# Making the high and low parts of a projection's weights in two halves of four blocks each

## The chip, the cores and the metric

The kernel runs on one core of one Trainium2 chip. The metric is device time of one execution in microseconds, here as the median of several runs; lower is better. TensorE (PE) multiplies, VectorE (DVE) and ScalarE (ACT) do elementwise work, GpSimd (POOL) does some of it, and SyncE (SP) issues most of the DMAs.

## The reference

One block of a sequence model in fp32, with 1024 positions of width 1024 and a depth of 1:

```
hn = rms_norm(x, norm_mix_g)
u = hn @ w_in                                  # 1024 x 7864
u_mla, u_fox, u_ssm, u_gate = split(u)
y_a = mla_branch(u_mla, ...) @ w_br_mla        # 8 heads, latent attention
y_b = fox_branch(u_fox, ...) @ w_br_fox        # 8 heads, attention with a forget gate
y_c = ssm_branch(u_ssm, ...) @ w_br_ssm        # conv of xBC, state space scan, 16 heads
g = sigmoid(u_gate + b_gate).reshape(B, S, 3, D)
merged = g[:, :, 0] * y_a + g[:, :, 1] * y_b + g[:, :, 2] * y_c
x = x + merged @ w_out
x = x + conv_ffn(rms_norm(x, norm_ffn_g), ...) # two projections of width 2816, a conv, a gate
```

## The kernel before, in words

**Products of fp32.** Each fp32 operand is split into a high part in fp32r and a low part, the raw value minus the high part, and a product is made of three matmuls: high by high, high by low, low by high. For weights, ACT copies the raw tile `wr` to the high tile `wh`, and DVE subtracts, `wl = wr - wh`.

**Stages.** Up to about 389 us the kernel normalises the input and makes those columns of `hn @ w_in` that the attention needs. Then the 16 attention heads run, up to about 908 us, and the chunks of the state space scan (SSD), up to about 1113 us. Branch outputs, merge, `w_out` and the feed-forward block follow.

**The fill.** The columns of `w_in` that attention doesn't need (12 blocks of 128 columns for the convolution, 24 for the gates) are projected by `all_fill` (L1157 to L1189). A block is two halves of 24 matmuls, 128x512 (L1174), into two alternating PSUM tiles `mm`; then ACT takes the result, with a plain copy (L1179) for a convolution block or a tanh (L1153) for a gate. The convolution's taps `t` follow on DVE (L1132 and others). The fill's matmuls are dealt out between those of the attention heads, and later between those of the SSD chunks, two of the eight k-blocks at a time, by `merge` and `advance`, which always advance the stream that is least far.

**The weights of a block.** `fill_load` (L1108 to L1119) is called for block n + 1 when block n starts. It issues the load of 128x1024 values (eight k-blocks of 128) into one of two `wr` tiles, and takes one of two `wh` and `wl` tiles. For blocks 0 and 1 the split is made at once. For the other 34 the copy (L1117) and the subtraction (L1118) are put into a queue with due times.

**The queue.** The order of all engines in these stages is written by a clock of costs: each step of a stream adds its estimated TensorE time to `clk`. `later(us, fn)` puts an instruction in the queue, due `us` after the present clock; `run_until` emits those that are due, by their due time; `force(h)` emits the queue up to handle `h`, when a buffer is wanted again or a block's weights are needed. `rl[0]`, which `fill_load` returns, is the handle of the last step that reads the raw tile and is forced before the block's matmuls. `pin` keeps an instruction in this order against its neighbours that are pinned too; the compiler's scheduler places the rest, so that a change of one step can swap others.

**What stands around it.** In attention, per row of 128 queries: scores `s` (L1291) into three alternating PSUM tiles; row maxima `nmx` (L1296 for a first chunk, L1307 for the last, L1309 joins two) on DVE; exponentials `pm` (L1314) on ACT; the row sum's reciprocal (L1319, L1320) on DVE, and the normalisation (L1321) on POOL. The probabilities are transposed (`tp`, L1379), copied by ACT to high parts `pth` (L1384) and by DVE to low parts `ptl` (L1385), and multiplied with the values into `o` (L1344 to L1352). ACT copies half of `o` out (L1357), and DVE adds the other half (L1362), which frees the PSUM region that the next values write. In the SSD chunks PE transposes through one PSUM tile `stp` (x at L1516, y at L1620); ACT copies it out (`xT` L1517, `yT` L1621), makes the decays `E` (L1548, L1549) and their high parts `Eh` (L134), and DVE the low parts `El` (L135) for the products `py` (L1584).

Of the kernel before, what the change touches and what calls it, by code (L numbers as in the profile page):

```python
# [15 lines left out]
AF = mybir.ActivationFunctionType  # L16
# [21 lines left out]
def f32(ap):  # L38
    return ap.bitcast(F32)
# [3 lines left out]
def block_kernel(ctx: ExitStack, tc: tile.TileContext, x, positions, norm_mix_g, w_in, b_gate,  # L43
# [5 lines left out]
    V, A, G, T, SY = nc.vector, nc.scalar, nc.gpsimd, nc.tensor, nc.sync  # L49
# [77 lines left out]
    def uid(s):  # L127
        cnt[0] += 1
        return f"{s}_{cnt[0]}"

    def split(h, l, src, he=None, le=None):
        he = he or A
        le = le or V
        i = A.activation(h, src, AF.Copy) if he is A else he.tensor_copy(h, src)  # L134
        return i, le.tensor_sub(l, src, f32(h))  # L135
# [8 lines left out]
    def pin(ins):  # L144

        i = ins.ins
        if i.engine in tail:
            tc.add_manual_dep(i, tail[i.engine],
                              mybir.DependencyInfo(mybir.DependencyClass.NoSync, mybir.DependencyReason.DATA),
                              reason="pin")  # L150
        tail[i.engine] = i.name
        return ins
# [918 lines left out]
    def later(us, fn):  # L1071
        h = [clk[0] + us, uid(""), fn]
        queue.append(h)
        return h
# [31 lines left out]
    pin = tc.keep_in_program_order  # L1106

    def fill_load(c0, now=False):  # L1108
        raw, rl = f_wr.get()
        SY.dma_start(raw, w_inv[:, :, c0:c0 + P])  # L1110
        h, _ = f_wh.get()
        l, _ = f_wl.get()
        if now:
            split(h, l, raw)
            rl[0] = None
            return h, l, rl
        later(4.0, lambda: pin(A.activation(h, raw, AF.Copy)))  # L1117
        rl[0] = later(5.3, lambda: pin(V.tensor_sub(l, raw, f32(h))))  # L1118
        return h, l, rl  # L1119

    def conv_done(j, u, ul, t0):
# [35 lines left out]
    def all_fill():  # L1157

        conv = [("c", j, C_XBC + j * P) for j in range(12)]
        gates = [(b, j, C_G + b * D + j * P) for b in (1, 0, 2) for j in range(NK)]  # L1160
        blocks = [e for n in range(12) for e in (conv[n], gates[n])] + gates[12:]
        nxt = fill_load(blocks[0][2], True)
        for n, (kind, j, c0) in enumerate(blocks):
            wh, wl, rl = nxt
            if n + 1 < len(blocks):
                nxt = fill_load(blocks[n + 1][2], n == 0)
            force(rl[0])
            u, ul = f_t4.get()
            for half in range(2):
                ps, pl = f_ps.get()  # L1170
                hs = slice(512 * half, 512 * half + 512)
                for k in range(NK):
                    for i, (a, b) in enumerate(((wh, hnh), (wh, hnl), (wl, hnh))):
                        T.matmul(ps, a[:, k, :], b[half][:, k, :], start=(k == 0 and i == 0),  # L1174
                                 stop=(k == NK - 1 and i == 2))
                    if (k + 1) % grain[0] == 0 and k < NK - 1:
                        yield 0.65 * grain[0]
                if kind == "c":
                    fn = lambda ps=ps, hs=hs, u=u: A.activation(u[:, hs], ps, AF.Copy)  # L1179
                else:  # L1180
                    fn = lambda ps=ps, hs=hs, u=u, r=8 * kind + j: gate_tanh(u[:, hs], ps, pc_g[:, r:r + 1])
                wait = 50.0 if n == len(blocks) - 1 and half == 1 else 0.0
                pl[0] = later(wait + 1.4, fn)
                if half == 1:
                    if kind == "c":
                        conv_done(j, u, ul, 2.2)
                    else:
                        ul[0] = later(wait + 2.0, lambda u=u, g=g_d[kind][j]: SY.dma_start(g, u))
                yield 0.65 * grain[0]  # L1189
# [461 lines left out]
    with ExitStack() as pe_:  # L1651
# [9 lines left out]
        def ops_tile(i):  # L1661
            return [mps[i // 4].tile([P, S], F32R, name=uid(n), tag=f"{n}{i}") for n in ("ah", "al")]

        for b, wsrc, nk in ((1, w_br_fox, 4), (0, w_br_mla, 4), (2, w_br_ssm, 8)):
# [3 lines left out]
            for k in range(nk):  # L1668
                if b == 1 and k < 2:
                    raw = frp.tile([P, 2, 512], F32, name=uid("ar"), tag=f"ws{k}").rearrange("p a s -> p (a s)")  # L1670
                else:
                    raw = fpl.tile([P, S], F32, name=uid("ar"), tag="t4", bufs=4)
                i = SY.dma_start(raw, ys_d[k] if b == 2 else att_d[b][k * P:k * P + P, :])
                if b == 1 and k < 2:
                    behind_(i, ys_stores[4])
                if b == 1:
                    h, l = fox_hl[k]
                else:
                    h, l = ops_tile(4 + k if b == 0 else k)
# [140 lines left out]
    for nh in range(2):  # L1820
        hl = []
        for kk in range(2):
            h, l = (ops[4 if nh else 2 * kk + i].tile([P, 4, 512], F32R, name=uid(n), tag=f"{n}{nh}{kk}")
                    for i, n in enumerate(("woh", "wol")))
            hl.append((h, l))
            for k in range(0, 4, 2):
                late = nh == 0 and kk == 1
                raw = fpl.tile([P, 2, 512], F32, name=uid("raw"), tag="t4" if late else "wr", bufs=4 if late else 2)
# [26 lines left out]
    for t, nh in units:  # L1855
        ns = slice(512 * nh, 512 * nh + 512)
        if nh == 0 and 4 <= t < 4 + FIRST:
# [10 lines left out]
            else:  # L1868
                raw = fpl.tile([P, NK, P], F32, name=uid("wr"), tag="t4", bufs=4)
# [249 lines left out]
    for pi, name in enumerate(steps):  # L2119
# [6 lines left out]
        for k in range(NFH):  # L2126
# [14 lines left out]
            for m, j in todo:  # L2141
                h, l = loaded[pi * NFH + j]
# [55 lines left out]
```

## Time and profile before

| | |
|---|---|
| runs | 2030.01, 2022.77, 2022.13 us |
| median of the runs | 2022.77 us |
| the profiled execution | 2026.82 us, its span 2025.1 us, mean granted clock 0.997 |
| busy: PE, DVE, ACT, POOL | 1997.5, 1382.0, 934.8, 651.1 us |
| DMA | 304.13 MB, mean 150 GB/s |

The profile is of one execution. The span runs from its first to its last recorded instruction; the execution's own time has 1.7 us around it. Rows of the timeline give start and duration in microseconds from the span's start, then engine, line, operation, output and inputs by the program's names. An instruction's duration can overlap the next one's start, so the distance between two starts is what one costs its engine in a row of them. Idle time ahead of an instruction stands in brackets with what released it. "PEclk" is the granted TensorE clock as a share of full speed.

### The profile page before, as it was taken

Reading aid. Unit: us, or ns where it says so; the run is one execution under the profiler, and the core shown is the slowest. Engines: PE = TensorE matmul, PEld = TensorE weight load, DVE = VectorE, ACT = ScalarE, POOL = GpSimd, SP = SyncE. Lnnn points to the kernel's source line nnn. Section 1 sums busy time; section 2 is a strip of 40 time slices with the busy share of each in tenths; the row PEclk is TensorE's granted clock in tenths of the full one; section 3 lists DMA queues with packets and bytes.
Section 4 is the critical chain, followed back from the end, with each engine's and each line's share of the span. In section 5 each row is a group of like instructions: output and inputs, shape, how many; then the busy total and the mean of one; then the engine's idle time right before and its main releaser. Section 6 shows DMA issues by size and latency. Waiting matters only on the chain. (4 is left out here: it accounts for less than half of the span.)

```text
span 2025.1 us, 28777 instructions
## 1 busy us (share of the span) xinstructions
PE 1997.5 (99%) x10189; PEld 1681.6 (83%) x10189; DVE 1382.0 (68%) x2410; ACT 934.8 (46%) x1700; POOL 651.1 (32%) x640
## 2 busy tenths in 40 slices
PE   8999999999999999999999999999999999999999
PEld 8999788888888888888777878888778888888887
DVE  7777567267666676657885556558997777675665
ACT  5555323255555556546665222324454444454432
POOL 5133322021222322213332063100555444522655
PEclk9999999999999999999999999999999999999999
DMA  6166857543535445424443678342322211249575
GB/s 176 51 193 217 267 174 217 170 125 102 140 116 140 125 112 155 116 74 142 131 137 128 220 243 291 136 135 83 115 87 90 84 63 42 84 137 329 204 259 193
DMA packets 276539, 304.13 MB, mean 150 GB/s; under 512 B 19070, under 2 KB 209546, under 8 KB 276395
## 3 DMA queue, kind: packets, MB, share of 16 engines
q1 hardware_dynamic: 276392, 302.29, 48.2%
q8 instruction: 80, 1.31, 0.3%
q14 instruction: 65, 0.52, 0.1%
q10 hardware_dynamic: 2, 0.00, 0.0%
HBM read 209.04 MB, written 93.19 MB: 149 GB/s over the span
## 5 line engine op out<-in xcount | busy, mean ns | idle before, releaser
L1321 POOL TENSOR_SCALAR pm<-pm,rs 128x128 f32<-128x128 f32 (+7 forms) x128 | 105.8, 829 | 415.4 <-DVE rs L1320 294.2
L1174 PE MATMUL mm<-hnh,wh 128*128 128x512 f32 x576 | 238.0, 413 | 0.0
L1174 PE MATMUL mm<-hnh,wl 128*128 128x512 f32 x576 | 226.5, 393 | 0.0
L1174 PE MATMUL mm<-hnl,wh 128*128 128x512 f32 x576 | 226.3, 393 | 0.0
L2145 PE MATMUL dn<-dr,dr 128*128 128x512 f32 x592 | 182.3, 389 | 0.0
L1314 ACT ACTIVATE pm<-s,nmx 128x128 f32<-128x128 f32 (+2 forms) x192 | 110.4, 581 | 65.3 <-DVE nmx L1309 61.8
L2145 PEld LDWEIGHTS dn<-dr,dr 128*128 128x128 f32 x592 | 111.1, 188 | 23.1
L1174 PEld LDWEIGHTS mm<-hnh,wl 128*128 128x128 f32 x576 | 108.4, 188 | 24.9
L1174 PEld LDWEIGHTS mm<-hnl,wh 128*128 128x128 f32 x576 | 109.2, 190 | 16.4 <-issue 0.5
L1174 PEld LDWEIGHTS mm<-hnh,wh 128*128 128x128 f32 x576 | 109.2, 190 | 16.3 <-issue 0.7
L1385 DVE TENSOR_TENSOR ptl<-tp,pth 128x512 fp32r<-128x512 f32 (+1 forms) x160 | 98.4, 632 | 33.0 <-ACT pth L1384 30.8
L1384 ACT ACTIVATE pth<-tp 128x512 fp32r<-128x512 f32 (+1 forms) x160 | 84.8, 555 | 72.6 <-PE tp L1379 72.5
L2145 PE MATMUL dn<-dr 128*128 128x512 f32 x296 | 115.2, 389 | 0.0
L135 DVE TENSOR_TENSOR dr<-dr,dr 128x1024 fp32r<-128x1024 f32 x52 | 75.3, 1459 | 48.3 <-ACT dr L134 35.6
L188 PE MATMUL ybr<-al,wh 128*128 128x512 f32 x256 | 99.4, 390 | 1.2 <-DVE al L1682 1.0
L188 PE MATMUL ybr<-ah,wh 128*128 128x512 f32 x256 | 98.9, 390 | 1.1 <-ACT ah L1681 0.9
L188 PE MATMUL ybr<-ah,wl 128*128 128x512 f32 x256 | 98.9, 390 | 0.0
L1307 DVE TENSOR_REDUCE nmx<-s 128x1 f32<-128x384 f32 (+3 forms) x128 | 65.8, 518 | 32.8 <-PE s L1291 19.2
L134 ACT ACTIVATE dr<-dr 128x1024 fp32r<-128x1024 f32 x52 | 54.8, 1061 | 71.6 <-PE dn L2145 55.0
L1379 PE MATMUL tp<-ident,pm 128*128 128x128 f32 x576 | 79.8, 273 | 0.6 <-POOL pm L1321 0.6
L135 DVE TENSOR_TENSOR wl<-S,wh 128x1024 fp32r<-128x1024 f32 x42 | 63.2, 1504 | 23.5 <-ACT wh L134 23.5
L134 ACT ACTIVATE wh<-wr 128x1024 fp32r<-128x1024 f32 (+1 forms) x40 | 35.0, 876 | 93.9 <-PE ybr L188 47.1
(528 smaller groups left out, 5853.3 us busy)
## 6 DMA issues: line engine op xcount, KB each, us to landing
dr<-act_d SPq DMA_DIRECT2D x99, 256.0 KB
wr<-in_w_in_dram SPq DMA_DIRECT2D x36, 512.0 KB
g_d<-t SPq DMA_DIRECT2D x24, 512.0 KB
gl<-g_d SPq DMA_DIRECT2D x24, 512.0 KB
wr<-in_ffn_w_up_dram SPq DMA_DIRECT2D x23, 512.0 KB
ws<-in_ffn_w_down_dram SPq DMA_DIRECT2D x22, 512.0 KB
wsum_d<-ws SPq DMA_DIRECT2D x22, 512.0 KB
act_d<-fa SPq DMA_DIRECT2D x22, 512.0 KB
```

The costliest lines, as they stand in the source:

```text
L134: i = A.activation(h, src, AF.Copy) if he is A else he.tensor_copy(h, src)
L135: return i, le.tensor_sub(l, src, f32(h))
L188: T.matmul(ps, a(k), b(k), start=(i == 0), stop=(i == n - 1))
L1174: T.matmul(ps, a[:, k, :], b[half][:, k, :], start=(k == 0 and i == 0), stop=(k == NK - 1 and i == 2))
L1307: V.reduce_max(nmx[:, ci:ci + 1], ps[:, :b - a], axis=AX, negate=True)
L1314: pss[cj][1][0] = later(t0 + 0.9 + 0.1 * cj, lambda cj=cj, a_=a_, b_=b_: A.activation(p_[:, a_:b_], pss[cj][0][:, :b_ - a_], AF.Exp, bias= ...
L1321: G.tensor_scalar(p_[:, 0:n * P], p_[:, 0:n * P], rs[:, 3:4], 0.0, op0=ALU.mult, op1=ALU.add)
L1379: T.transpose(pt[:, off:off + P], pn[qi][0][:, k * P:k * P + P], ident)
L1384: later(cs + 0.05, lambda th=th, pt=pt, off=off: A.activation(th[:, :off], pt[:, :off], AF.Copy))
L1385: pl[0] = later(cs + 0.6, lambda th=th, tl=tl, pt=pt, off=off: V.tensor_sub(tl[:, :off], pt[:, :off], f32(th[:, :off])))
L2145: T.matmul(ps[m], a[:, ts_], b[:, 512:], start=first_ and j == 0 and q == 0, stop=j == NFH - 1 and q == 2, skip_group_check=not first_)
```

## The change

The copy and the subtraction of a block's weights are each made in two halves of four k-blocks (512 of the 1024 values of a partition). The copies are due at +4.0 and +5.2 us of the order's clock and the subtractions at +5.0 and +6.2 us; `rl[0]` is the second subtraction. The loads, tiles and matmuls are the same, and so are the splits of blocks 0 and 1.

```
-        later(4.0, lambda: pin(A.activation(h, raw, AF.Copy)))
-        rl[0] = later(5.3, lambda: pin(V.tensor_sub(l, raw, f32(h))))
+        for i in range(2):
+            ks = slice(4 * i, 4 * i + 4)
+            later(4.0 + 1.2 * i, lambda ks=ks: pin(A.activation(h[:, ks, :], raw[:, ks, :], AF.Copy)))
+            rl[0] = later(5.0 + 1.2 * i, lambda ks=ks: pin(V.tensor_sub(l[:, ks, :], raw[:, ks, :], f32(h[:, ks, :]))))
```

After the change the copy is L1119, the subtraction L1120, and lines behind them have numbers that are higher by two. The steps move on their engines as follows. The first place is at about 541 us of the profile of before, in the attention stage. ACT before (the outputs are the high weights `wh`, output halves `o` and probabilities `pm`):

```order
L1314 ACTIVATE pm_6452,rs_6454<-s_6455,nmx_6453 128x512
L1314 ACTIVATE pm_6452,rs_6454<-s_6498,nmx_6453 128x384
L1117 ACTIVATE wh_6481<-wr_6479 128x1024
L1357 ACTIVATE o_1675_6525<-o 64x256
L1357 ACTIVATE o_1684_6552<-o 64x256
L1314 ACTIVATE pm_6513,rs_6515<-s_6516,nmx_6514 128x512
L1314 ACTIVATE pm_6513,rs_6515<-s_6543,nmx_6514 128x512
L1384 ACTIVATE pth_6576<-tp_6571 128x512
L1384 ACTIVATE pth_6583<-tp_6578 128x512
```

ACT in the same place after the change (each name's last number is another, since more names are drawn):

```order
L1316 ACTIVATE pm_6464,rs_6466<-s_6467,nmx_6465 128x512
L1316 ACTIVATE pm_6464,rs_6466<-s_6510,nmx_6465 128x384
L1119 ACTIVATE wh_6493<-wr_6491 128x512
L1359 ACTIVATE o_1689_6537<-o 64x256
L1119 ACTIVATE wh_6493<-wr_6491 128x512
L1359 ACTIVATE o_1698_6565<-o 64x256
L1386 ACTIVATE pth_6590<-tp_6585 128x512
L1386 ACTIVATE pth_6597<-tp_6592 128x512
L1316 ACTIVATE pm_6525,rs_6527<-s_6528,nmx_6526 128x512
L1316 ACTIVATE pm_6525,rs_6527<-s_6556,nmx_6526 128x512
```

The first copy of `o` stands behind half a split and ahead of the other half, and the two `pth` copies now stand ahead of the two exponentials of 128x512.

DVE at that place before, from a tap of the convolution on (`nmx` are row maxima, `o` the sum of the two output halves, `t` taps):

```order
L1132 SCALAR_TENSOR_TENSOR t_1624_6440<-t_1545_6238,pc_g,t_1624_6440 128x512
L1307 TENSOR_REDUCE nmx_6514<-s_6543 128x1
L1362 TENSOR_TENSOR o_1676_6526<-o,o_1675_6525 64x256
L1118 TENSOR_TENSOR wl_6482<-wr_6479,wh_6481 128x1024
L1309 TENSOR_TENSOR nmx_6514<-nmx_6514 128x1
L1132 SCALAR_TENSOR_TENSOR t_1624_6440<-t_1545_6238,pc_g,t_1624_6440 128x510
L1307 TENSOR_REDUCE nmx_6564<-s_6566 128x1
L1362 TENSOR_TENSOR o_1685_6553<-o,o_1684_6552 64x256
```

DVE there after the change:

```order
L1134 SCALAR_TENSOR_TENSOR t_1636_6452<-t_1557_6248,pc_g,t_1636_6452 128x512
L1364 TENSOR_TENSOR o_1690_6538<-o,o_1689_6537 64x256
L1120 TENSOR_TENSOR wl_6494<-wr_6491,wh_6493 128x512
L1309 TENSOR_REDUCE nmx_6526<-s_6556 128x1
L1120 TENSOR_TENSOR wl_6494<-wr_6491,wh_6493 128x512
L1309 TENSOR_REDUCE nmx_6578<-s_6580 128x1
L1364 TENSOR_TENSOR o_1699_6566<-o,o_1698_6565 64x256
L1311 TENSOR_TENSOR nmx_6526<-nmx_6526 128x1
```

The first sum comes ahead of the row maximum that stood before it, one maximum stands between the two half subtractions, and the joined maximum (`nmx` from `nmx`) comes last of these.

The second place is at about 1031 us, in an SSD chunk. ACT before (`E` are decays, `yT` the transposed output of the chunk):

```order
L134 ACTIVATE Eh_12188<-E_12184 128x512
L1153 ACTIVATE t_3862_12156<-mm_12157,pc_g 128x512
L134 ACTIVATE Eh_12206<-E_12202 128x512
L1548 ACTIVATE E_12214<-pse_12211 128x512
L1621 ACTIVATE yT_12023<-stp_12246 128x512
L1549 ACTIVATE E_12214<-E_12214 128x512
```

ACT there after the change:

```order
L134 ACTIVATE Eh_12248<-E_12244 128x512
L1155 ACTIVATE t_3924_12216<-mm_12217,pc_g 128x512
L134 ACTIVATE Eh_12267<-E_12263 128x512
L1119 ACTIVATE wh_12214<-wr_12212 128x512
L1550 ACTIVATE E_12275<-pse_12272 128x512
L1623 ACTIVATE yT_12083<-stp_12308 128x512
L1551 ACTIVATE E_12275<-E_12275 128x512
```

The second half of a block's copy stands between a copy of `Eh` and the decay ahead of `yT`; before, the whole copy stood eleven rows above the first of these.

## The prediction

> **What bounds the kernel now.** I read the busy line of the page first, then a table of stages, then what TensorE waited for in the two stages that the change touches, and last the places of those waits in the timeline. The busy line:
>
> ```profile
> PE 1997.5 (99%) x10189; PEld 1681.6 (83%) x10189; DVE 1382.0 (68%) x2410; ACT 934.8 (46%) x1700; POOL 651.1 (32%) x640
> ```
>
> TensorE is busy for 99% of the span. The fill, in whose course all the changed splits stand, runs from 389.4 to 1112.6 us, as one row of the fill's own line shows (count, shortest, median and longest ns, first and last start):
>
> ```profile
> L1174 PE MATMUL mm<-hnh,wh x576: 387/396/796, 389.4 to 1112.6; 128*128 128x512 f32 x192
> ```
>
> It has an attention stage, to 908 us, and an SSD stage. The rows of the table of stages (start and end, length, then busy time of PE, its weight loads, DVE, ACT and POOL, granted clock, DMA share, GB/s):
>
> ```profile
> 389.00:908.00 519.00, 515.25 (x3033) 440.22 (x3031) 341.06 (x793) 285.96 (x707) 121.75 (x143) 1.00 0.45 123
> 908.00:1113.00 205.00, 201.60 (x1041) 162.01 (x1042) 153.38 (x249) 125.05 (x202) 63.22 (x80) 0.99 0.43 133
> ```
>
> TensorE stands still for 519.00 − 515.25 = 3.75 us in attention and 205.00 − 201.60 = 3.40 us in SSD. No edit to VectorE or ScalarE work can give back more than about these 7.2 us, so the question is which of them the splits cause. The waits of TensorE by releaser (total us, times, longest), attention first, then SSD:
>
> ```profile
> PE o L1344 <- DVE o L1362: 1.6, 1, 1.6
> PE s L1291 <- ACT pm L1314: 0.9, 1, 0.9
> PE tp L1379 <- POOL pm L1321: 0.6, 1, 0.6
> ```
>
> ```profile
> PE stp L1516 <- ACT yT L1621: 1.5, 2, 1.2
> PE stp L1516 <- DVE o L1362: 0.9, 1, 0.9
> PE py L1584 <- ACT E L1548: 0.8, 1, 0.8
> PE stp L1620 <- ACT y L1612: 0.7, 1, 0.7
> ```
>
> Each is a single event or two. No row names a split (`wh`, `wl`) as what TensorE waited for. A split can cause such a wait only by standing ahead of the named instruction on its engine.
>
> **The fixed cost of two halves.** Groups of the whole run (operation, shapes, count, busy us, mean ns of one, idle time before):
>
> ```profile
> L1117 ACT ACTIVATE wh<-wr 128x1024 fp32r<-128x1024 f32 x34 | 35.9, 1055 | 0.0
> L1118 DVE TENSOR_TENSOR wl<-wr,wh 128x1024 fp32r<-128x1024 f32 x34 | 41.7, 1226 | 1.0 <-ACT wh L1117 1.0
> L134 ACT ACTIVATE Eh<-E 128x512 fp32r<-128x512 f32 x32 | 20.0, 628 | 12.3 <-DVE E L1550 11.3 <-PE py L1584 0.9
> L135 DVE TENSOR_TENSOR El<-E,Eh 128x512 fp32r<-128x512 f32 x32 | 21.9, 688 | 6.8 <-ACT Eh L134 6.2
> ```
>
> The last two are the same operations at the new size. A pair of half copies takes 2 x 628 − 1055 = 201 ns more than one whole copy, a pair of half subtractions 2 x 688 − 1226 = 150 ns more: over 34 blocks 6.8 us more on ACT and 5.1 us more on DVE. Both lie beside matmuls: in the attention row ACT is busy for 286 of 519 us and DVE for 341. I cost them at nothing except where the engine is saturated just ahead of a wait; if the cover were gone, 201 + 150 = 351 ns a block would be exposed, 34 x 0.351 = 11.9 us in all. On this the Trainium skill, page "VectorE: DVE Perf Modes", section "The TRN2 errata", speaks against the change: one large tile pays the access latency once, many small ones pay it per tile, and by its formula for an fp32 tensor_tensor the halves would take 691 ns each against 1224 ns; the rows above agree within 3 ns, and by its price the DVE term would be 158 ns a block, 5.4 us over 34.
>
> **The second half is later.** Its copy is due at +5.2 us and its subtraction at +6.2 us of the order's clock, where the whole ones had +4.0 and +5.3. The block with the least room, in one row of DVE and one of PE:
>
> ```profile
> 899.39 1.22 DVE L1118 TENSOR_TENSOR wl<-wr,wh 128x1024 fp32r<-128x1024 f32 x1
> ```
>
> ```profile
> 905.06 0.40 PE L1174 MATMUL mm<-hnh,wh 128*128 128x512 f32 x1
> ```
>
> The split ends at 900.61 and its block starts at 905.06: 4.45 us of room for a shift of about one, so no matmul waits for weights and this term is zero. No load starts later either: SP's loads go out at the block's start, and a raw buffer freed one microsecond later is loaded a block afterwards.
>
> **The place where a half helps.** The longest wait of attention, ACT and DVE first, then PE (start us, duration, engine, line, operation, in brackets the idle time and its releaser):
>
> ```profile
> 541.09 1.05 ACT L1117 ACTIVATE wh<-wr 128x1024 fp32r<-128x1024 f32 x1
> 542.17 0.38 ACT L1357 ACTIVATE o<-o 64x256 f32<-64x256 f32 x1
> 541.51 0.73 DVE L1132 SCALAR_TENSOR_TENSOR t<-t,pc_g,t 128x512 f32<-128x512 f32 x1
> 542.16 0.68 DVE L1307 TENSOR_REDUCE nmx<-s 128x1 f32<-128x512 f32 x1
> 542.76 0.41 DVE L1362 TENSOR_TENSOR o<-o,o 64x256 f32<-64x256 f32 x1
> 543.09 1.21 DVE L1118 TENSOR_TENSOR wl<-wr,wh 128x1024 fp32r<-128x1024 f32 x1
> 544.22 0.15 DVE L1309 TENSOR_TENSOR nmx<-nmx 128x1 f32<-128x1 f32 x1
> 545.14 0.68 ACT L1314 ACTIVATE pm<-s,nmx 128x512 f32<-128x512 f32 x1
> ```
>
> ```profile
> 543.22 0.39 PE L1344 MATMUL o<-pth,vv 128*128 128x256 f32 x1 [1.55 <-DVE o L1362]
> 548.26 0.52 PE L1291 MATMUL s<-qk,qk 104*128 104x256 f32 x3
> ```
>
> The order of before put the whole copy ahead of the output copy L1357 and a row maximum ahead of the sum L1362. In the changed order only half a copy stands ahead of L1357, which then ends about 0.53 us earlier, and the sum comes directly behind the convolution tap: it starts at 542.16 instead of 542.76. **Gain: 0.60 us** at TensorE. What is late next is the row maximum L1309, now behind two half subtractions and two maxima (about 544.9 instead of 544.22), and its exponentials, which now stand behind two `pth` copies (about 1.2 us later). The next scores are at 548.26, some 2.5 us behind the end of these exponentials in before (545.14 + 0.68), so I cost that at nothing; if this cover were gone, up to 0.7 us of the 0.60 gained would be paid back.
>
> **The place where it costs in attention.** The second wait, 0.86 us before scores at 418.08:
>
> ```profile
> 413.22 1.21 DVE L1118 TENSOR_TENSOR wl<-wr,wh 128x1024 fp32r<-128x1024 f32 x1
> ...
> 417.01 0.14 DVE L1309 TENSOR_TENSOR nmx<-nmx 128x1 f32<-128x1 f32 x1
> ```
>
> ```profile
> 418.08 0.63 PE L1291 MATMUL s<-qk,qk 104*128 104x256 f32 x3 [0.86 <-ACT pm L1314]
> ```
>
> DVE runs without a gap from the subtraction to L1309, the exponential follows, and TensorE waits for it. Here both halves stand next to each other in the new order with the same instructions behind them, so the extra 0.15 us is exposed: **+0.15 us** (bounds 0 and 0.15). The third wait is for POOL, with no split ahead of it: 0.
>
> **The place where it costs in SSD.** The 1.2 us wait for `yT`:
>
> ```profile
> 1031.41 0.62 ACT L134 ACTIVATE Eh<-E 128x512 fp32r<-128x512 f32 x1
> 1031.93 0.59 ACT L1548 ACTIVATE E<-pse 128x512 f32<-128x512 f32 x1
> 1032.41 0.60 ACT L1621 ACTIVATE yT<-stp 128x512 f32<-128x512 f32 x1
> ```
>
> ```profile
> 1033.06 0.95 PE L1516 MATMUL stp<-ident,t 128*128 128x128 f32 x4 [1.18 <-ACT yT L1621]
> ```
>
> ```profile
> 541.00:545.00 4.00, 2.45 (x20) 1.98 (x18) 3.76 (x10) 2.44 (x6) 1.34 (x1) 1.00 0.92 255
> 1033.00:1037.00 4.00, 3.94 (x13) 3.26 (x14) 3.97 (x8) 1.76 (x4) 0.00 (x0) 0.57 0.63 173
> ```
>
> In before the whole copy stood fourteen rows ahead of this `E`. Now its second half stands between the `Eh` at 1031.41 and the `E` at 1031.93. ACT has no gap there, so `yT` ends one half copy later: **+0.60 us** (0.53 by the spacing of the rows, 0.63 by the duration; I take the middle). After this wait the granted clock falls to 0.57 for four microseconds, 0.43 x 4 = 1.7 us lost already in before. A longer wait may prolong that or draw a second drop, between 0 and +1.7 us; I take 0, since the longer wait at 543 (1.55 us) kept a clock of 1.00, in the upper of the two rows. In the next chunk a half also stands ahead of the same `E` and `yT`, where before shows no wait as long: 0 to +0.6, I take 0. The other SSD waits have no split moved to or from them: 0, with their own 2.4 us (0.9 + 0.8 + 0.7) as the lower bound.
>
> The scheduler also swaps neighbours elsewhere (value copies ahead of exponentials in the forgetting heads, reciprocals and maxima on DVE, stores and head loads on SP; on PE three transposes behind four fill matmuls near 903, whose results are used 4 us later). None stands at a listed wait: 0, between −0.6 and +0.9 by the sizes of the listed attention waits.
>
> **The sum.** −0.60 + 0.15 + 0.60 = +0.15 us on the profiled execution's 2026.82 us, 2026.97. That execution lies 4.05 us above the median of the runs (2022.77), so on the scale of the median the forecast is 2022.9 us. No change that can be measured.
>
> **The rivals.** *A, faster: the splits are behind most of the idle time.* The page "Perfetto Trace Analysis" of the Trainium skill, section "Optimizing Scalar/DVE Operations", says that breaking up instructions may let work finish sooner when these engines aren't saturated but cause bubbles elsewhere; it is this rival's rule, and the rows bear it out at one wait, that at 543. If the listed waits went, 3.1 + 3.9 = 7.0 us, and with them the clock loss of 1.7: 2022.77 − 8.7 = 2014.1 us. Against it: of the eight events only those at 543 and 418 have a split ahead of them without a gap.
>
> *B, slower: the second half pushes the row maxima.* Each split of attention now comes in two visits to DVE, and maxima that stood behind one subtraction may stand behind an extra half. One half subtraction of 0.688 us, exposed at each of the 24 attention splits, is 16.5 us: 2039.3 us. It decides when a score bank's room is under 0.69 us at most of these splits. Against it: only the 0.9 us wait at 418 shows a score matmul without room; the 22 splits elsewhere (without 413 and 543) stand beside no listed wait. For it: DVE has 178 us free in attention, but in gaps.
>
> *C, slower: the fixed cost is exposed throughout.* That needs ACT and DVE to set TensorE's pace block by block: +11.9 us, 2034.7 us. Against it: a TensorE idle for 0.7% of the attention stage.
>
> That the change does nothing is excluded by the order: 34 more instructions stand on each of the two engines, all 68 of half size.
>
> **How the numbers follow.** Forecast 0.82, A 0.09, B 0.05, C 0.04. The forecast's own range goes from all SSD and attention terms at their good ends (−3.0 − 0.6) to their bad ends with a clock drop (0.15 + 0.63 + 1.7 + 0.6 + 0.9 = +4.0), 2019 to 2027 us; three runs of before reached from 2022.13 to 2030.01, so a median may lie some microseconds higher. The range of 2015 to 2031 holds that and most of A; B and C are left out. Half a per cent, 10.1 us, is about what a measurement of this kernel can tell from no change: faster is below 2012.7, slower above 2032.9. A reaches the first only with more than the listed waits (0.02), B and C and a sliver of the forecast lie beyond the second (0.09); 0.89 remain for the same.
>
> **What would show it.** Right: two groups of 68 at about 630 and 690 ns, the wait at 543 down to about 0.95 us, the one near 1033 up to about 1.8, idle time of TensorE in both stages within 2 us of 3.75 and 3.40. Wrong: many new waits of `s` for `pm` (B), TensorE's busy time unchanged and some 0.35 us idle at each split (C), or idle time near zero in both (A).

## The result, and the profile after

| | before | after |
|---|---|---|
| median of 22 runs each, us | 2024.95 | 2028.14 |
| lowest to highest, us | 2020.67 to 2030.91 | 2025.36 to 2033.11 |
| the profiled execution, us | 2026.82 | 2030.61 |

The ratio is 1.0018, 95% interval 1.0011 to 1.0026: the changed kernel is slower by 2 to 5 us. Forecast were 2022.9 us and a change of +0.15 us. The time lies in the range and within half a per cent, but the size of the change, about three microseconds, came from terms that the sum had at zero. Of the 5.2 us between the forecast and the measured median, 2.2 are the kernel before itself: its median is 2024.95 us in 22 runs, and was 2022.77 in the first three.

Two stretches of the trace can be compared without the rest of the run: **attention**, from the fill's first matmul to the first SSD transpose, and **SSD**, from there to the fill's last matmul. The boundaries, first of the kernel before (its fill's row stands in the prediction), then of the changed one:

```profile
908.47 0.33 PE L1516 MATMUL stp<-ident,t 128*128 128x128 f32 x1 [0.92 <-DVE o L1362]
```

```profile
L1176 PE MATMUL mm<-hnh,wh x576: 387/396/796, 387.4 to 1115.6; 128*128 128x512 f32 x192
...
904.96 0.33 PE L1518 MATMUL stp<-ident,t 128*128 128x128 f32 x1 [0.92 <-DVE o L1364]
```

Attention took 908.47 − 389.4 = 519.1 us before and 904.96 − 387.4 = 517.5 after: **1.6 us gained**. SSD took 204.6 before (to the start of the fill's last matmul, at 1113.0) and 211.1 after (to 1116.0): **6.5 us lost**. Together that is 4.9 us in this one pair of executions, against 3.2 us between the medians, so a part of the 6.5 us belongs to the two executions. The waits of TensorE after, attention (387 to 905 us), then SSD (to 1116):

```profile
PE o L1346 <- DVE o L1364: 1.0, 1, 1.0
...
PE s L1293 <- ACT pm L1316: 0.9, 2, 0.6
```

```profile
PE py L1586 <- ACT E L1550: 1.7, 1, 1.7
PE stp L1622 <- ACT yT L1623: 1.5, 1, 1.5
PE stp L1518 <- ACT yT L1623: 1.3, 2, 1.0
PE py L1586 <- DVE y L1590: 1.0, 1, 1.0
PE stp L1518 <- DVE o L1364: 0.9, 1, 0.9
PE stp L1622 <- ACT y L1614: 0.4, 1, 0.4
```

The SSD waits add up to 6.8 us, before to 3.9. At three of them the granted clock fell. The rows of the three stretches (the third number from the end is the clock):

```profile
930.00:936.00 6.00, 4.95 (x21) 4.13 (x21) 3.91 (x10) 3.46 (x7) 0.88 (x1) 0.72 0.01 3
1006.00:1012.00 6.00, 4.76 (x16) 3.95 (x17) 5.54 (x10) 4.87 (x9) 0.00 (x0) 0.72 0.23 73
1076.00:1082.00 6.00, 4.32 (x17) 3.53 (x17) 5.93 (x12) 5.12 (x10) 0.00 (x0) 0.75 0.15 45
```

Each drop costs about 0.28 x 6 = 1.7 us. Before there was one in the SSD stage, after three: 3.4 us more. Together, 2.9 us of waits and 3.4 us of clock, that is 6.3 of the 6.5 us.

**Where the wait at 1007 comes from.** The wait of 1.5 us stands at 1007 us, where before has none. ACT and PE there after:

```profile
1001.82 1.15 ACT L1614 ACTIVATE y<-y,yr 128x1024 f32<-128x1024 f32 x1 [3.44 <-POOL yr L180]
...
1006.61 0.58 ACT L1623 ACTIVATE yT<-stp 128x512 f32<-128x512 f32 x1
```

```profile
1007.24 1.10 PE L1622 MATMUL stp<-ident,y 128*128 128x128 f32 x4 [1.51 <-ACT yT L1623]
```

No split stands in this stretch. ACT's scaling of `y` waited 3.44 us for `yr`, the last step of an inverse square root on POOL, and the chunk's decays and `yT` were queued behind it. POOL there, of the kernel before and then after:

```profile
998.23 1.91 POOL L1536 TENSOR_TENSOR xdd<-xT,dend 128x1024 f32<-128x1024 f32 x1
1000.12 0.27 POOL L180 TENSOR_SCALAR yr<-rg_t,yr 128x1 f32<-128x1 f32 x1
1000.34 1.90 POOL L1538 TENSOR_TENSOR y<-xT,Db 128x1024 f32<-128x1024 f32 x1
```

```profile
997.26 1.91 POOL L1538 TENSOR_TENSOR xdd<-xT,dend 128x1024 f32<-128x1024 f32 x1
999.12 1.90 POOL L1540 TENSOR_TENSOR y<-xT,Db 128x1024 f32<-128x1024 f32 x1
1001.01 0.78 POOL L180 TENSOR_SCALAR yr<-rg_t,yr 128x1 f32<-128x1 f32 x1
```

The scheduler had put a product of 1.90 us ahead of a step of 0.27 us. The change touches neither; that the halves had shifted the scheduler's own timeline is inferred.

**The wait of 1.7 us near 1078** has the same chain without a swap: in both kernels `yr` stands behind both products there. ACT before, then after:

```profile
1071.53 1.15 ACT L1612 ACTIVATE y<-y,yr 128x1024 f32<-128x1024 f32 x1 [2.25 <-POOL yr L180]
```

```profile
1072.98 1.15 ACT L1614 ACTIVATE y<-y,yr 128x1024 f32<-128x1024 f32 x1 [3.02 <-POOL yr L180]
```

`yr` ran for 0.82 us there instead of 0.27, and the wait for `E` behind it grew from 0.8 to 1.7 us, with a drop of the clock at it. Why that step ran longer was not looked into.

### The profile page after: what moved, and what is told of

Same layout as the page of the kernel before. It is cut to its first block, busy times and chain, and to the rows that moved or that the text cites. A ratio compares the mean times of both kernels' runs of the same rounds, so it can differ in the third digit from the quotient of the medians.

```text
span 2028.8 us, 28842 instructions
## 1 busy us (share of the span) xinstructions
PE 1997.9 (98%) x10189; PEld 1681.7 (83%) x10189; DVE 1383.1 (68%) x2444; ACT 939.3 (46%) x1734; POOL 659.1 (32%) x640
```

## The experiments

Two theories were tried. **O**: the loss comes from the new order in the SSD stage (and what follows from it), and attention gains. **F**: two instructions for one cost more, and the cost is exposed at all 34 splits. The ratios are against the kernel before on the same chip; lengths are those of the one profiled execution, SSD from the first transpose to the start of the fill's last matmul, and "clock" is what the granted clock took from SSD, (1 − clock) x length over stretches of 2 us.

| kernel | ratio, 95% interval | attention us | SSD us | clock us |
|---|---|---|---|---|
| before | 1 | 519.1 | 204.6 | 1.7 |
| after | 1.0018 (1.0011 to 1.0026) | 517.5 | 211.1 | 5.1 |
| 1 halves in attention | 0.9998 (0.9990 to 1.0006) | 517.4 | 204.1 | 0 |
| 2 halves in SSD | 1.0033 (1.0021 to 1.0045) | 519.0 | 209.4 | 3.4 |
| 3 after, POOL rule | 1.0001 (0.9992 to 1.0010) | 517.5 | 208.3 | 5.1 |
| 4 before, POOL rule | 0.9994 (0.9985 to 1.0004) | 519.1 | 203.2 | 1.7 |
| 5 halves in attention, POOL rule | 0.9986 (0.9976 to 0.9996) | 517.5 | 205.7 | 3.4 |
| 6 halves in SSD, POOL rule | 1.0008 (0.9996 to 1.0020) | 520.6 | 205.0 | 1.7 |
| 7 whole, later | 1.0021 (1.0013 to 1.0030) | 517.1 | 212.4 | 6.8 |
| 8 adjacent halves in attention | 1.0006 (0.9998 to 1.0015) | 520.2 | 202.9 | 0 |
| 9 copy halved, attention | one run | 518.3 | 204.0 | 0 |
| 10 subtraction halved, attention | one run | 518.9 | 205.4 | 1.7 |
| 11 as 5, xd rule | 0.9990 (0.9977 to 1.0002) | 517.4 | 203.4 | 0 |
| 12 as 3, xd rule | 0.9983 (0.9973 to 0.9992) | 517.4 | 203.1 | 0 |

The 520.6 of the sixth holds a clock drop of 1.7 us behind the wait near 543.

**1 and 2: one stage each.** The split takes either form by a count of the calls; in the second the comparison is `> 24`:

```
+        seen[0] += 1
+        if seen[0] <= 24:
+            # the two halves of the change
+        else:
+            # the whole copy and subtraction of before
```

> Halves only for the 24 splits of the attention stage; the ten of the SSD stage whole, whose order on every engine is then that of before. Theory O (the loss is made by the new order of the SSD stage, and attention gains at the 543 wait): TensorE's idle time from the fill's start to the end of attention about 1 us less than before, SSD as before, so 0.5 to 1.5 us faster than before (ratio 0.9993 to 0.9998). Rival F (the fixed cost of two halves is exposed evenly at the 34 splits): 24/34 of the 3.2 us lost remain, +2.3 us (ratio 1.0011).

> The counterpart: halves only for the ten splits of the SSD stage; the attention stage has the order of before. Theory O: the whole loss of the SSD stage, 4 to 6 us slower than before (ratio 1.002 to 1.003), with stalls of over 1 us ahead of the py and stp matmuls and a drop of the granted clock behind them. Rival F: 10/34 of the loss, +0.9 us (ratio 1.0005).

Measured: 0.9998 and 1.0033. The first keeps the whole gain in attention (517.4 us) and has the SSD order of before (204.1 us; ACT's `y` near 996 waits 1.33 us for `yr`, as in before). The second has 209.4 us of SSD, with the swap (3.46 us near 1004), and loses more than the change itself. So the halves of the SSD stage bring the swap. By F the first would be slower than the second; it is the other way round. The interval of the first holds 1, so its gain is seen only in the trace, where attention is 1.7 us shorter.

**3 and 4: POOL's order.** `last_yr` is set at each step of the inverse square root:

```
-            G.tensor_mul(o.y, xv, Db.unsqueeze(2).to_broadcast([P, 16, 64]))
+            g_ = G.tensor_mul(o.y, xv, Db.unsqueeze(2).to_broadcast([P, 16, 64]))
+            if last_yr[0] is not None:
+                behind_(g_, last_yr[0])
```

`behind_` makes the scheduler put the product behind that step, without a semaphore.

> The changed kernel with one rule more: on POOL the product y<-xT,Db of a chunk stands behind the last yr of the chunk ahead of it. In the changed kernel it had come ahead of that yr in the fifth chunk, and ACT's scaling of y waited 3.4 us for yr with the decays and yT queued behind it. Theory O: the 1.5 us stall ahead of stp near 1007 and its clock drop are gone, 2 to 3 us faster than the changed kernel, 0 to 1.5 us slower than before. Rival F: nothing gained, as the changed kernel (+3.2 us against before).

> The kernel before with the same rule for POOL's order, splits whole. Theory O: it takes away the waits of ACT's scaling of y for yr that before has too (TensorE waited 0.7 us for y and 0.8 us for E), so 0 to 1.5 us faster than before. Rival F says nothing of it: no change.

In the third the ratio falls from 1.0018 to 1.0001, as O has it, and the wait at 1007 is gone. Not all of this 0.0017 need be the price of the swap: the same rule takes the kernel before from 1 to 0.9994, which is not clear of no change, and with the rule in both kernels the halves cost 0.0007, by intervals that overlap. POOL and ACT at that place:

```profile
997.02 1.90 POOL L1540 TENSOR_TENSOR xdd<-xT,dend 128x1024 f32<-128x1024 f32 x1
998.91 0.27 POOL L182 TENSOR_SCALAR yr<-rg_t,yr 128x1 f32<-128x1 f32 x1
999.13 1.90 POOL L1542 TENSOR_TENSOR y<-xT,Db 128x1024 f32<-128x1024 f32 x1
```

```profile
999.21 1.15 ACT L1618 ACTIVATE y<-y,yr 128x1024 f32<-128x1024 f32 x1 [1.33 <-POOL yr L182]
```

But its profiled execution still has 208.3 us of SSD. What is late next is `yT` of the following chunk (waits of the third, then of the fourth):

```profile
PE stp L1520 <- ACT yT L1627: 2.8, 2, 2.5
PE py L1590 <- DVE y L1594: 1.0, 1, 1.0
```

```profile
PE stp L1518 <- ACT yT L1625: 1.9, 2, 1.6
```

In both the waits for ACT's `E` and `y` (0.8 and 0.7 us before) are gone. The wait for `yT` near 1033, where half a copy stands in the third and none in the fourth, is 2.5 us against 1.6: 0.9 us more, of which the half copy was forecast to make 0.6. In the third, DVE's `xd` also ran for 2.93 us in the chunk ahead of it (at 1017) instead of 1.21, so that not all of it need be the half copy's. Taken over all profiles the slow `xd` looks like the larger part: this wait is 2.4 to 2.5 us in the three that have it (3, 6 and 7, the last without halves) and 0.9 to 1.6 in the other eleven; and in 11 and 12, both with an `xd` of 1.2 us there, it is 0.86 us without the half copy and 1.12 with it. Of the third's 208.3 us, 5.1 are the clock's.

**5 and 6: the rule with halves in one stage.** They join the edits of 1 and 4, and of 2 and 4.

> Halves in attention alone, as in the first experiment, together with the rule for POOL's order of the third and fourth. Theory O: both gains add: about 0.6 us at the output wait of attention, and the waits for y and E in SSD gone, 1 to 3 us faster than before (ratio 0.9985 to 0.9995). Rival F: +2.3 us as the halves of attention cost, less what the rule gives.

> Halves in SSD alone with the rule for POOL's order. Theory O: what the rule takes away is most of the loss of halves in SSD (6.6 us by the second experiment); what is left is the half copy ahead of E and yT near 1033 and the races of DVE and POOL: 0 to 2 us slower than before. Rival F: 10 splits at 0.35 us, +3.5 us by the fixed cost, and the rule changes nothing: 4 to 6 us slower.

The fifth, 0.9986, is faster than both kernels. In the sixth the rule takes the loss of SSD halves from 1.0033 to 1.0008; its interval holds no change.

**7: the same delay without halves.**

```
-        later(4.0, lambda: pin(A.activation(h, raw, AF.Copy)))
-        rl[0] = later(5.3, lambda: pin(V.tensor_sub(l, raw, f32(h))))
+        later(5.2, lambda: pin(A.activation(h, raw, AF.Copy)))
+        rl[0] = later(6.2, lambda: pin(V.tensor_sub(l, raw, f32(h))))
```

> No halves: whole copy and whole subtraction, only due 1.2 and 0.9 us later (at +5.2 and +6.2, the times of the second halves). Theory O: place and not size counts. The output copy now stands ahead of the split's copy near 541, so that wait shrinks by 0.6 us or more without any halving; and the new order of the SSD stage, with POOL's yr behind y<-xT,Db in another chunk, moves the SSD waits by one to several us in either direction. Rival F: no second instruction, no fixed cost: as before within 1 us, and the wait near 543 at 1.6 us.

This is the sharpest of them. Without one instruction more it gains as much in attention (517.1 us) and loses more in SSD (212.4 us): 1.0021. ACT near the wait that stood at 543:

```profile
535.04 0.38 ACT L1357 ACTIVATE o<-o 64x256 f32<-64x256 f32 x1
535.33 1.04 ACT L1117 ACTIVATE wh<-wr 128x1024 fp32r<-128x1024 f32 x1
```

```profile
PE o L1344 <- DVE o L1362: 1.0, 1, 1.0
```

The output copy stands ahead of the whole split, and the wait is 1.0 us, as with halves. So the place made the gain. In SSD it has three drops of the clock, one of them twice as long, 6.8 us in all, and waits for `yT` of 3.7 us in two. F has no term for it. But POOL's swap isn't there (ACT's `y` near 1001 waits 1.33 us, as in before): `xd` was slow, 2.9 us, in three of the eight chunks, and each of the three drops stands at a wait that follows one of these. So a later place can cost SSD in more than one way, and how much of that is the order and how much the execution was not separated.

**8: the fixed cost alone.** Two halves, both due at +4.0 and +5.3, in attention only.

> Halves in attention alone, both due at the times of the whole split (+4.0 and +5.3), so that the two halves stand next to each other where the whole one stood: the fixed cost without the new places. Theory O: the wait near 543 stays at 1.6 us, the one near 418 grows by 0.1 to 0.2 us; 0 to 0.5 us slower than before. Rival F: 24 x 0.35 us at most, 2 to 8 us slower.

The halves stand next to each other where the whole split stood. The wait near 543 is 1.6 us again, and the stage takes 520.2 us, 1.0 more than before, without a drop of the clock. Counted at the first matmul of every block the lag grows evenly, 0.39 us at the eighth and 0.83 at the twenty-first: about 0.043 us a split. Of the 0.35 us of more work a split that the prediction worked out, an eighth reaches TensorE. Neither theory had this: O expected at most 0.5 us, F at least 2. F is true in kind: as an estimate, 34 x 0.043 = 1.5 us of its 11.9, more than the 0 of the prediction's sum. The ratio's interval, 0.9998 to 1.0015, holds that and no change.

**9 and 10: one engine each, in attention.** The copy in halves with a whole subtraction at +6.2, and the whole copy at +4.0 with halved subtractions:

> Attention alone: only ACT's copy in two halves (+4.0 and +5.2), the subtraction whole, due at +6.2; SSD whole as before. If the gain of attention (519.1 to 517.5 us from the fill's first matmul to the first SSD transpose) comes from the output copy, and with it the output sum, being earlier on ACT and DVE, this has most of it: 517 to 518 us, the wait near 543 at 1.0 us. Rival, that the halved subtraction frees DVE for the maxima: it has nothing, 519 us.

> The counterpart: only DVE's subtraction in two halves (+5.0 and +6.2), the copy whole at +4.0. By the first theory no gain: 519 us or slightly more, the wait near 543 at 1.6 us, the one near 418 up to 0.15 us longer. By the rival the whole gain, 517 to 518 us.

Waits of the ninth, then of the tenth:

```profile
PE s L1301 <- ACT pm L1324: 1.8, 3, 0.9
PE o L1354 <- DVE o L1372: 1.0, 1, 1.0
```

```profile
PE o L1354 <- DVE o L1372: 1.6, 1, 1.6
PE s L1301 <- ACT pm L1324: 1.2, 2, 0.9
```

The copy alone takes the wait for `o` to 1.0 us, the subtraction alone does not. But there are 1.8 us of waits for `pm`, against 0.9 with both halved; the longest, 0.91 us near 876, has the whole subtraction, now later, ahead of row maxima. So the ninth has half the gain (518.3 us), and my expectation of most of it was too high.

**11 and 12: keeping DVE's `xd` ahead of POOL's `xdd`.** Both read `xT` at the start of a chunk.

```
-            V.tensor_mul(xd, xv, hb(dt, c))
+            x_ = V.tensor_mul(xd, xv, hb(dt, c))
+            dc = pool.tile([P, 16], F32, name=uid("dc"), tag="dc")
+            behind_(V.tensor_copy(dc, dend[:, c, :]), x_)
...
-            G.tensor_mul(o.xdd, xv, hb(dend, c))
+            G.tensor_mul(o.xdd, xv, dc.unsqueeze(2).to_broadcast([P, 16, 64]))
```

> Halves in attention with POOL's order rule, and DVE's xd kept ahead of POOL's xdd in each SSD chunk: xdd reads its decay factors from a small copy (128x16) that DVE makes directly behind xd. If the 1.05 us stall ahead of py near 930 comes from xd running for 2.9 us instead of 1.2 beside POOL's xdd, all eight xd are at 1.2 us and that stall is gone: 1 to 2 us faster than the fifth experiment where the race was lost, 3 to 5 us faster than before (ratio 0.9975 to 0.9985). If the stall has another cause, as the fifth experiment (ratio 0.9986) or slower by what xdd comes later.

> The changed kernel, halves everywhere, with both rules. If new order and races are all that the halves of SSD cost, it has the gain of attention and an SSD stage near that of before (205 us), 1 to 4 us faster than before (ratio 0.998 to 0.9995). If the halves themselves cost SSD, an SSD stage of 207 us or more and no gain against before.

As a test of the race this failed. With `xdd` held back the scheduler let POOL's other product start there, and the second chunk's `xd` was slow again (2.88 us in the eleventh); the wait of `py` for `y` stayed at 1.0 us. POOL of the eleventh:

```profile
923.58 1.90 POOL L1550 TENSOR_TENSOR y<-xT,Db 128x1024 f32<-128x1024 f32 x1 [12.69 <-ACT xT L1527]
926.82 1.90 POOL L1548 TENSOR_TENSOR xdd<-xT,dc 128x1024 f32<-128x1024 f32 x1 [1.34 <-DVE dc L1546]
```

As kernels they answer another question. With both rules SSD takes 203.4 us with whole splits (11) and 203.1 with halves (12), one execution each: in this order the halves cost SSD nothing that shows. The twelfth, 0.9983, is the best measured; its interval overlaps the fifth's, so which is faster is open.

## Why the prediction held its range and missed its size

The prediction's own worst case, all its terms at their bad ends, reached 2027 us; the measured 2028.14 lies above it. That the range of 2015 to 2031 held is owed to the margin left for the spread of runs, not to the sum, and is luck as far as the mechanism goes.

*The wait at 543: −0.60 forecast.* Right, by the mechanism named. DVE and PE after:

```profile
540.19 0.41 DVE L1364 TENSOR_TENSOR o<-o,o 64x256 f32<-64x256 f32 x1
540.53 0.67 DVE L1120 TENSOR_TENSOR wl<-wr,wh 128x512 fp32r<-128x512 f32 x1
541.12 0.68 DVE L1309 TENSOR_REDUCE nmx<-s 128x1 f32<-128x512 f32 x1
...
543.00 0.14 DVE L1311 TENSOR_TENSOR nmx<-nmx 128x1 f32<-128x1 f32 x1
```

```profile
540.65 0.39 PE L1346 MATMUL o<-pth,vv 128*128 128x256 f32 x1 [0.96 <-DVE o L1364]
```

The wait is 0.96 us for 1.55. The joined maximum came 2.35 us behind this matmul (before: 1.00), and no score matmul waited for it, as forecast.

*The wait at 418: +0.15 forecast.* Wrong in sign: 0.60 us for 0.86. From the subtraction to the joined maximum DVE took 0.06 us more (3.85 for 3.79 us), less than forecast; but the sum of the outputs ahead of it, and so the whole chain, came earlier. I had looked only downstream of the split. The listed waits of attention fell by 0.6 us in all (2.5 for 3.1). The other 1.0 us of its gain grows bit by bit up to about 870 us, without a wait of TensorE that the profile lists; its cause was not shown.

*The wait at 1033: +0.60 forecast.* The half copy stands where the order had it, and yet the wait is 1.02 us for 1.18:

```profile
1033.24 0.62 ACT L134 ACTIVATE Eh<-E 128x512 fp32r<-128x512 f32 x1
1033.76 0.62 ACT L1119 ACTIVATE wh<-wr 128x512 fp32r<-128x512 f32 x1
1034.28 0.58 ACT L1550 ACTIVATE E<-pse 128x512 f32<-128x512 f32 x1
1034.76 0.59 ACT L1623 ACTIVATE yT<-stp 128x512 f32<-128x512 f32 x1
```

TensorE itself arrived later, held up at 1007. Once that wait was taken away (3 against 4) the wait near 1033 was 0.9 us longer with the half copy, in which a slow `xd` has a part; where `xd` ran for 1.2 us in both kernels (12 against 11) it was 0.26 us longer. So the 0.60 looks too large, though no experiment moved the half copy alone.

*The scheduler's swaps: "None stands at a listed wait: 0".* **This is the step that failed.** A swap needs no wait of before to make one: POOL's swap stood at a place without any and made 1.5 us there. Behind the zero lay the sentence that a split can cause a wait only by standing ahead of the named instruction on its engine; here no split stands ahead of it at all. I had gone through the waits of before and asked what moved at them; the new order on POOL, read for itself, shows a long product ahead of a short step on which ACT's queue hangs. With the rule against it the changed kernel is level with the kernel before (1.0001). The longer wait near 1078, put down to nothing too, went with the same rule.

*The clock: 0 taken, 0 to +1.7 us as bounds.* Too narrow: two more drops, 3.4 us. A drop isn't a fixed companion of a wait, as the first experiment has the 1.2 us wait near 1033 without one, and before has it with one. In these two stages of the 14 profiles, 17 of the 36 waits of 1.0 us or more have a drop at them, and none of the 88 shorter ones that the profile lists; there is no other drop. More long waits mean more chances.

*The fixed cost: 0 taken.* 0.043 us a split in attention by the eighth experiment's trace. The groups after:

```profile
L1120 DVE TENSOR_TENSOR wl<-wr,wh 128x512 fp32r<-128x512 f32 x68 | 49.5, 736 | 0.2
L1119 ACT ACTIVATE wh<-wr 128x512 fp32r<-128x512 f32 x68 | 41.8, 624 | 0.0
```

A half subtraction takes 736 ns in the mean for the 688 forecast: DVE's busy time for them is 7.8 us more, for 5.1.

Of the rivals, A was right that placement can win time and wrong in its price (1.6 us in attention, not 7.0), B made one short wait (0.30 us for `pm`, near 878), C holds for about an eighth by that estimate. Of the signs of being right, the one on idle time failed in SSD: TensorE stood still for 6.0 us there, more than 2 us above 3.40.

## What to carry over

Where a scheduler orders the engines by its own timeline, an edit of work that is off the critical path is first of all a new order: compare the orders of every engine, the untouched ones too, and look for long instructions that have come ahead of short ones on which another queue hangs. Try the same delay without the edit before you credit the edit, and pin the one order that matters. A wait costs more than its length when the clock may drop at it, here by 1.7 us, and twice by 3.4, at 17 of 36 waits of 1.0 to 2.5 us.

## What the runs showed of the hardware

**A collision of DVE and POOL goes either way.** In the second chunk both start on `xT` within 0.03 us. DVE, then POOL, of the kernel before:

```profile
929.70 1.21 DVE L1534 TENSOR_TENSOR xd<-xT,dt 128x1024 f32<-128x1024 f32 x1
```

```profile
929.67 3.00 POOL L1536 TENSOR_TENSOR xdd<-xT,dend 128x1024 f32<-128x1024 f32 x1 [13.09 <-ACT xT L1517]
```

And after:

```profile
926.16 2.95 DVE L1536 TENSOR_TENSOR xd<-xT,dt 128x1024 f32<-128x1024 f32 x1
```

```profile
926.13 1.91 POOL L1538 TENSOR_TENSOR xdd<-xT,dend 128x1024 f32<-128x1024 f32 x1 [12.71 <-ACT xT L1519]
```

One runs at its usual length (1.21 us on DVE, 1.91 on POOL) and the other takes nearly as long as both together (3.00 and 2.95). The Trainium skill, "Perfetto Trace Analysis", section "Optimizing Scalar/DVE Operations", says that GpSimd and DVE share an SBUF read port; these rows agree. DVE lost in 11 of the 14 profiles, and in these TensorE waited 1.0 to 1.6 us for `y` near 930; in the other three (before, 4 and 8) it did not. Before and 1 have the same SSD order, and 1 has this wait, so of the 6.5 us lost this 1 us, and the 1.7 us of the drop at it, belong to the execution as much as to the change. That the lost race causes the wait was not shown, since the experiment that should have ended it did not.

**The clock fell at waits of 1.0 to 2.5 us.** On the page "TensorE: Matmul & The Clock Gate", Part 1, "The HAM clock gate", the Trainium skill gives an idle window of about 3.4 us as what brings the clock down. Here waits of 1.05 (at 932), 1.51 and 1.68 us each had a clock of 0.5 at them that took 1.7 us, so for about 3.4 us, while an equal wait of 1.05 us in the first experiment had none; the measurement decides.
